# Preparing the mixer's and the second feed-forward's weights inside the first feed-forward's input stage

## The chip, the cores and the metric

The kernel runs on one NeuronCore of a Trainium2 chip. The metric is device time of one execution in microseconds; the figure of a kernel is the median of repeated runs. Five engines work beside each other and meet only through semaphores: TensorE (PE: matrix products), VectorE (DVE), ScalarE (ACT), GpSimd (POOL) and SyncE (SP, which here only issues DMAs). POOL issues DMAs too. Each engine executes its own list of instructions in the order in which the build wrote it: an instruction that waits holds up all that stand behind it on that engine.

## The reference

One encoder layer on x of 1024 tokens by 1024 features, in float32: two feed-forwards (SwiGLU, inner width 2816) with a token mixer between them. Each sub-layer computes `LN(ALPHA*x + w*(1+gate)*f(x*(1+scale)+shift))` where shift, scale and gate come from a small conditioning product. Cut to what matters here:

```python
def swiglu(h, w_in, w_out):
    gate, up = jnp.split(h @ w_in, 2, axis=-1)
    return (jax.nn.silu(gate) * up) @ w_out

def hybrid_mixer(h, w_in, ..., w_out, ...):
    proj = h @ w_in                      # 1024 x 2560 columns
    glu_a, glu_b, q, k, v = split(proj)  # 512 columns each
    conv_out = silu(LN(depthwise_conv31(glu_a * sigmoid(glu_b)) + conv_b))
    # 4 heads: a = softmax(q1 k1) - lam * softmax(q2 k2); rms_norm(a @ v)
    attn_out = diff_attention(q, k, v, ...)
    return concat([conv_out, attn_out]) @ w_out   # 1024 x 1024
```

## The kernel before

Every float32 operand of a large product is split into two parts of the 32-bit format that TensorE takes at one column per step (`F32R`): a high part, written by a cast on ACT, and a low part, the operand less its high part, by a subtraction on DVE (`split`, L141 and L142). A product is then three matmuls (high*high, high*low, low*high). The feed-forwards' products are also cut by a scheme of Strassen's kind: seven half-size products instead of eight, on sums of quarters of the weights (S1 to S4) and of the activations (T1 to T4).

The stages follow each other: the start (0 to 75 us); the input product of feed-forward 1, in 22 blocks of 128 inner columns (to 490.8); its output product (to 706); the mixer's projections, GLU, k, q and v, with the width-31 convolution on DVE beside them (to 950); attention in 8 query tiles by 4 heads (to 1150); the mixer's output product (to 1242); feed-forward 2's input product (to about 1690) and output product.

In `in_phase`, block j runs seven products in the order 1, 2, 6, 5, 7, 3, 4, each of 12 matmuls, and evacuates each from PSUM by DVE and ACT (`in_steps`: the evacuation of product 7 is L425, that of product 3 L428). During a block the next block's weights are loaded by SP, summed (`in_sums`, into tile `sf`), and split (`sh`, `sl`). After each block `hook(j)` does small jobs of the conditioning. After product 2 of the last block the output phase's first step, and after product 5 the second and third, are prepared ahead (`out_ahead`); `out_phase` goes on with steps of 12 matmuls `fo<-wr,gl` (L571), each of which needs a split weight piece `wr` and a split activation piece `gl`.

The projections load raw weights (`kr`, `qr`, `vr`, 512 KB each) and split them. `q_stack` makes the query tiles for the transposes on PE (`qTh` and `qTl`, L1057): its `qh` and its copy of `ql` are POOL instructions, behind the rotary embedding `rope` on the same engine. In attention a worker written as interleaved generators computes per iteration scores, softmax, the difference `p` (POOL, L1128 and L1129, or DVE, L1126), transposes `aT` and the product with v (L1146). `finish` normalises: `ss` on DVE (L1162), `pow` on POOL (L1165), `o` on DVE (L1168). `out_weights` loads a piece of the mixer's output weights, multiplies it with `gate1` (L1099, on POOL for the pieces loaded in attention) and splits it. `gate1` itself is accumulated in the first output phase (`ada_gate`, L155).

The order of feed-forward 2's first blocks is written out by hand in the string `MSEQ`: a token such as `r1G` (right-hand sums of quarter 1, engine G = POOL or V = DVE), `X0GV` and `x0V` (sums S1, S2 of block 0, and their split), `p01` (product 1 of block 0); a leading `!` ties a token to the matmuls before it.

Of the kernel before, what the change touches and what calls it, by code (L numbers as in the profile page):

```python
# [17 lines left out]
P = 128  # L18
T = 1024
# [19 lines left out]
MSEQ = "m5 G0 f0 r0V f1 d5 r1G !m6 f2 r2V f3 d6 r3G m7 d7 F0 !X0GV x0V | !Y0VG p01 p02 s0GV y0V F2 G1 t0V F1 s1VV t1G s2VV p11 !F3 !X1GV s3VV b0 t2V t3V u0GV b1 v0V u1GG v1V b2 b3 !p12 Y1GG u3VV u2GV v2V v3V x1V !p06 y1G p05 !p16 !p07 p15 !p03 !p17 p04 W0 p13 !p14"  # L39
# [11 lines left out]
def layer_kernel(ctx, tc, a, out):  # L51
# [55 lines left out]
    def late_consts(wp, tag, bufs):  # L107
        vec_raw = wp.tile([45, P], F32, tag=tag, bufs=bufs, name="vec_raw")
# [6 lines left out]
        SY.dma_start(cw_raw, a["conv_w"][0])  # L115
        cps = bank("consts_ps")
# [8 lines left out]
        SY.dma_start(ropec, a["rope"].rearrange("(t p) e i -> p t e i", p=P))  # L125
        lraw = wp.tile([P, 4, 64], F32, tag=tag, bufs=bufs, name="lraw")
        for n, nm in enumerate(("lambda_q1", "lambda_k1", "lambda_q2", "lambda_k2")):
            SY.dma_start(lraw[:, n], a[nm].partition_broadcast(P))
        V.tensor_tensor(lraw[:, 0], lraw[:, 0], lraw[:, 1], ALU.mult)
# [162 lines left out]
    def new_ops():  # L292
# [4 lines left out]
        "ra": ([P, 3, 4, P], 2), "rb": ([P, 4, P], 2), "ah": ([P, 3, 4, P], 2), "al": ([P, 3, 4, P], 2),  # L297
# [11 lines left out]
    def in_load(wp, s, w_in, j, q=SY):  # L309
        rp = raw_pool.get(s, wp)  # L310
        ra = rp.tile([P, 3, 4, P], F32, tag="ra", bufs=2, name=f"ra{s}_{j}")
        rb = rp.tile([P, 4, P], F32, tag="rb", bufs=2, name=f"rb{s}_{j}")
# [3 lines left out]
        for dst, src in ((ra[:, 0], k1[:, :, g]), (ra[:, 1], k2[:, :, g]), (rb, k1[:, :, u]), (ra[:, 2], k2[:, :, u])):  # L316
            q.dma_start(dst, src)
        return ra, rb

    def in_gate(wp, s, j, raws):  # L320
        ra, rb = raws
# [5 lines left out]
    def in_sums(wp, s, j, raws, left, eng=V, order=(0, 1)):  # L327
        ra, rb = raws
        if s == 2 and order == (0, 1) and j in (1, 2):
            eng = G  # L330
        if order[0] == 0:
            left["sf"] = [wp.tile([P, 2, 4, P], F32, tag="sf", bufs=2, name=f"sf{s}_{j}_{i}") for i in range(2)]
        sf = left["sf"]
        if 0 in order:
            eng.tensor_tensor(sf[0][:, 0], rb, ra[:, 2], ALU.add)
            eng.tensor_tensor(sf[0][:, 1], sf[0][:, 0], ra[:, 0], ALU.subtract)
        if 1 in order:
            eng.tensor_tensor(sf[1][:, 0], ra[:, 0], rb, ALU.subtract)
            eng.tensor_tensor(sf[1][:, 1], ra[:, 1], sf[0][:, 1], ALU.subtract)
        for i in order:  # L340
            sh = wp.tile([P, 2, 4, P], F32R, tag="sh", bufs=3, name=f"sh{s}_{j}_{i}")
            sl = wp.tile([P, 2, 4, P], F32R, tag="sl", bufs=3, name=f"sl{s}_{j}_{i}")
            last = split(sh, sl, sf[i])
            for e in range(2):
                left[f"S{2 * i + e + 1}"] = (sh[:, e], sl[:, e])
# [19 lines left out]
    late = []  # L365
    pe_last = []
# [7 lines left out]
    def in_steps(wp, s, j, L, ops, gd, begun={}):  # L374
# [32 lines left out]
        def p2():  # L407
            V.tensor_tensor(c0, prod("A12", "B21"), cp["p1"], ALU.add)  # L408
# [9 lines left out]
        def p5():  # L418
            cp["b"] = prod("S1", "T1")
            S.copy(temp("p5"), cp["b"])  # L420
# [6 lines left out]
        def p3():  # L427
            V.tensor_tensor(c1, prod("S4", "B22", cp["b"]), cp["u2"], ALU.add)  # L428
            S.activation(c1, c1, AF.Silu)
# [31 lines left out]
        def p4():  # L461
# [4 lines left out]
            V.tensor_tensor(c0, c0, c21, ALU.mult)  # L466
# [1039 lines left out]
```

## Time and profile before

| | |
|---|---|
| median of 3 runs | 1909.49 us (1908.7 to 1911.0) |
| the profiled execution | 1910.44 us, span 1908.6 us, so 1.84 us outside the span |
| mean granted clock of TensorE | 0.989 of full |
| PE busy | 1825.0 us, 96% of the span; 83.6 us idle |
| DVE / ACT / POOL busy | 1450.6 / 781.3 / 298.2 us |

The engine with the highest share is PE, and its idle time is small, so a change can win only what PE waits for (83.6 us at most) and what it loses at half its clock. The other engines matter where PE waits for one of them, and where one of them is so full that it would make PE wait if it got more to do.

### The profile page before, as it was taken

The numbers are of one execution on the slowest core, as the hardware profiler recorded it, in microseconds if no ns is written. First come the engines' busy times: TensorE is split into PE (matmuls) and PEld (weight loads), VectorE is DVE, ScalarE is ACT, GpSimd is POOL, SyncE is SP. The second block draws the span as 40 slices with busy tenths as digits, with TensorE's granted clock in tenths as the row PEclk, the third lists the DMA queues.
The fourth block names the chain that finished last, engine by engine and source line by source line (L and its number), as shares of the span: only waits on it lengthen the run. The fifth ranks groups of instructions, "written<-read, shape, count | busy, mean of one in ns | idle before, by whom it ended". The sixth has DMA issues, their size and how long they took to land. (4 is left out here: it accounts for less than half of the span.)

```text
span 1908.6 us, 23158 instructions
## 1 busy us (share of the span) xinstructions
PE 1825.0 (96%) x8570; PEld 1513.0 (79%) x8570; DVE 1450.6 (76%) x1952; ACT 781.3 (41%) x1270; POOL 298.2 (16%) x243
## 2 busy tenths in 40 slices
PE   5999999999999999999999789979999999999997
PEld 5788888888888878878788677857888888888886
DVE  4977767766698878999888768688777565569888
ACT  2633333333445442132277664353333333254540
POOL 0000000000000020057667541260000000000001
PEclk9999999999999999999999999989999999999999
DMA  9337445542885325110000014125555333178432
GB/s 311 95 120 224 157 149 177 165 139 90 307 300 157 106 61 166 44 41 27 11 1 1 12 45 154 67 67 170 165 173 180 121 115 123 43 280 284 128 121 72
DMA packets 203952, 246.77 MB, mean 129 GB/s; under 512 B 14378, under 2 KB 125087, under 8 KB 203838
## 3 DMA queue, kind: packets, MB, share of 16 engines
q1 hardware_dynamic: 198378, 234.76, 37.8%
q0 software_dynamic: 2112, 7.34, 1.0%
q10 hardware_dynamic: 3348, 3.18, 0.5%
q8 instruction: 67, 1.10, 0.2%
q14 instruction: 47, 0.39, 0.1%
HBM read 188.08 MB, written 57.15 MB: 128 GB/s over the span
## 5 line engine op out<-in xcount | busy, mean ns | idle before, releaser
L571 PE MATMUL fo<-wr,gl 128*128 128x512 f32 x1848 | 422.5, 390 | 0.5 <-DVE pv L614 0.4
L571 PEld LDWEIGHTS fo<-wr,gl 128*128 128x128 f32 x1848 | 346.2, 188 | 74.7 <-issue 1.0
L142 DVE TENSOR_TENSOR sl<-sf,sh 128x1024 fp32r<-128x1024 f32 x87 | 108.3, 1245 | 110.2 <-ACT sh L141 110.1
L141 ACT CAST sh<-sf 128x1024 fp32r<-128x1024 f32 x88 | 92.8, 1055 | 207.4 <-issue 23.7
L949 DVE SCALAR_TENSOR_TENSOR cacc<-u,convw,cacc 128x1009 f32<-128x1009 f32 (+14 forms) x120 | 151.5, 1324 | 0.2
L381 POOL DMA_DIRECT2D gd<-gf x8 | 4.6, 571 | 887.9 <-DVE gf L447 887.5
L142 DVE TENSOR_TENSOR gl<-gr,gl 128x512 fp32r<-128x512 f32 x148 | 102.1, 695 | 8.5 <-ACT gl L141 6.9
L141 ACT CAST gl<-gr 128x512 fp32r<-128x512 f32 x148 | 90.5, 617 | 24.4 <-DMA gr<-gd 17.6
L155 DVE SCALAR_TENSOR_TENSOR ada<-adaw,c_act,ada 128x512 f32<-128x512 f32 x98 | 73.3, 748 | 28.4 <-DMA adaw<-in_w_ada_dram 27.6
L1075 DVE TENSOR_REDUCE mx<-sc 128x1 f32<-128x1024 f32 x64 | 76.3, 1215 | 19.6 <-PE sc L1073 19.6
L1077 ACT ACTIVATE p<-sc,mx 128x1024 f32<-128x1024 f32 x64 | 71.6, 1121 | 44.7 <-DVE mx L1075 44.5
L141 ACT CAST ah<-ra 128x1536 fp32r<-128x1536 f32 x44 | 65.2, 1481 | 56.0 <-DMA ada<-in_w_ada_dram 12.2
L217 POOL TENSOR_TENSOR rr<-rv,mhalf 128x1 f32<-128x1 f32 x24 | 21.9, 911 | 410.0 <-DVE rv L215 410.0
L409 ACT ACTIVATE gf<-gf 128x512 f32<-128x512 f32 x44 | 27.8, 632 | 125.9 <-DVE gf L408 120.1
L142 DVE TENSOR_TENSOR al<-ra,ah 128x1536 fp32r<-128x1536 f32 x44 | 77.1, 1752 | 1.1 <-ACT ah L141 1.0
L141 ACT CAST wr<-wa 128x512 fp32r<-128x512 f32 x66 | 41.2, 624 | 74.0 <-PE fo L571 72.6
L930 PE MATMUL glu<-hm,gluh 128*128 128x512 f32 x256 | 65.6, 391 | 0.0
L142 DVE TENSOR_TENSOR wr<-wa,wr 128x512 fp32r<-128x512 f32 x66 | 45.6, 690 | 26.1 <-ACT wr L141 25.7
L1129 POOL TENSOR_TENSOR p<-p,p 128x1024 f32<-128x1024 f32 x27 | 65.0, 2408 | 1.8
L1146 PE MATMUL av<-vf,aT 128*128 128x128 f32 x512 | 64.2, 280 | 1.0 <-ACT cacc L1211 1.0
L141 ACT CAST wr<-wb 128x512 fp32r<-128x512 f32 x66 | 40.2, 621 | 60.0 <-PE fo L571 49.6
L1146 PEld LDWEIGHTS av<-vf,aT 128*128 128x128 f32 x512 | 61.3, 196 | 1.5 <-ACT cacc L1211 1.3
(3425 smaller groups left out, 4701.4 us busy)
## 6 DMA issues: line engine op xcount, KB each, us to landing
gr<-gd SPq DMA_DIRECT2D x148, 256.0 KB
ra<-in_ffn_w_in_dram SPq DMA_DIRECT2D x129, 256.0 KB
adaw<-in_w_ada_dram SPq DMA_DIRECT2D x56, 512.0 KB
gd<-gf SPq DMA_DIRECT2D x102, 256.0 KB
wb<-in_ffn_w_out_dram SPq DMA_DIRECT2D x44, 256.0 KB
wa<-in_ffn_w_out_dram SPq DMA_DIRECT2D x44, 256.0 KB
rb<-in_ffn_w_in_dram SPq DMA_DIRECT2D x43, 256.0 KB
gd<-s SPq DMA_DIRECT2D x40, 256.0 KB
```

Of the source, the lines that this page charges most:

```text
L141: a = S.copy(hi, x)
L142: b = eng.tensor_tensor(lo, x, hi.bitcast(F32), ALU.subtract)
L155: V.scalar_tensor_tensor(acc, raw[:, jj], c_act[:, n : n + 1], acc, ALU.mult, ALU.add)
L217: G.tensor_tensor(r, v, mhalf[:, 0:1], ALU.pow)
L409: S.activation(c0, c0, AF.Silu)
L571: PE.matmul(ps, lhsT=g[:, x, ts_], rhs=w[:, y], start=n in (1, 2, 3) and k == i == 0, stop=k == NK - 1 and i == 2, skip_group_check=n not ...
L930: PE.matmul(q[2 * m + h], lhsT=w[:, m * P : (m + 1) * P], rhs=hm[k][h][:, x], start=k == 0 and n == 0, stop=k == KD - 1 and n == 2,)
L949: V.scalar_tensor_tensor(acc[:, lo_t:hi_t], u[:, lo_t + sh : hi_t + sh], convw[:, i, jj : jj + 1], acc[:, lo_t:hi_t], ALU.mult, ALU.add,)
L1075: V.tensor_reduce(mx_, ps, axis=AX.X, op=ALU.max, negate=True)
L1077: S.activation(pe, ps, AF.Exp, bias=mx_, accum_out=sm[:, e : e + 1])
L1129: last = G.tensor_tensor(p0, p0, p1, ALU.add)
L1146: PE.matmul(ps[:, 0:P], lhsT=aT[:, kt], rhs=vf[kt][:, h * P : (h + 1) * P], start=kt == 0, stop=kt == 7)
```

## The change

It prepares pieces of later weights during blocks 2 to 21 of the first input stage and keeps the results in DRAM. There are 48 units of 128 rows by 512 columns: 24 of the mixer's k, q and v columns, 16 halves of its output weights (multiplied by `gate1`), and 8 pieces of the sums S1 to S4 for blocks 0 and 1 of feed-forward 2. A unit is loaded into one of two buffers `mw`, changed in place, cast (ACT), subtracted (DVE) and stored; loads and stores are issued by POOL. Two units are loaded after each of blocks 1 to 10, none after 11, one after 12, and from block 13 one after product 5 and two at the block's end; they are worked off at the next such place.

Later the split pairs are loaded from DRAM by SP: 24 loads of 512 KB in place of 12 for k, q and v, 8 of 1 MB each for the output weights (two of 512 KB per piece) in place of raw pieces of 512 KB, and 6 of 512 KB for the sums (tokens `S0`, `S1`, `T1` in `MSEQ`). The splits and gate multiplications there go, and so do tile `sf` and the sums' own instructions.

The rest: the first stage's sums are made in place in one tile `r4`; `late_consts` is spread over blocks 11 to 13; `gate1` is accumulated after blocks 3 and 5 and no longer in the output phase; the rotary embedding of query tile 0 is on DVE, its `qh` on ACT and both halves of `ql` on DVE; the small `ss` operation of `finish` and its like in `conv_stat` go from DVE to POOL; in `MSEQ` the right-hand sums and splits `r1`, `r3`, `t1` and the second operand of `s0` go from POOL to DVE.

```diff
-MSEQ = "m5 G0 f0 r0V f1 d5 r1G !m6 f2 r2V f3 d6 r3G m7 d7 F0 !X0GV x0V | !Y0VG p01 p02 s0GV y0V F2 G1 t0V F1 s1VV t1G ...
+MSEQ = "m5 G0 f0 r0V f1 d5 r1V !m6 f2 r2V f3 S0 d6 r3V m7 d7 F0 | p01 p02 s0VV F2 G1 t0V F1 s1VV t1V ... T0 S1 ...
...
+        if s == 0:
+            for i in order:
+                if i == 0:
+                    eng.tensor_tensor(ra[:, 2], rb, ra[:, 2], ALU.add)
+                    eng.tensor_tensor(rb, ra[:, 0], rb, ALU.subtract)
+                    eng.tensor_tensor(ra[:, 0], ra[:, 2], ra[:, 0], ALU.subtract)
+                else:
+                    eng.tensor_tensor(ra[:, 1], ra[:, 1], ra[:, 0], ALU.subtract)
...
+        hook(1)
         for j in range(2, NJ):
...
             for n in (1, 2, 6, 5, 7, 3, 4):
                 st[n]()
+                if n == 5 and mid_hook:
+                    mid_hook(j)
...
             hook(j)
+        hook(NJ)
...
+        def mix_part():
+
+            t, dst, *hs = loaded.pop(0)
+            with tc.issue_after(pace["V"]), tc.issue_after(pace["S"]):
+                if hs and hs[0] is None:
+                    sums_of(t[:, 0].rearrange("p (s n) -> p s n", s=4))
+                elif hs:
+                    V.tensor_tensor(t[:, 0], t[:, 0], mods["gate1"][:, hs[0]], ALU.mult)
+                S.copy(t[:, 1].bitcast(F32R), t[:, 0])
+                V.tensor_tensor(t[:, 0].bitcast(F32R), t[:, 0], t[:, 1], ALU.subtract)
+            if hs and hs[0] is None:
+                for x in range(2):
+                    G.dma_start(dst[:, x], t[:, x].rearrange("p (s n) -> p s n", s=4))
+            else:
+                G.dma_start(dst, t)
...
+            pieces({11: 0, 12: 1}.get(j, 2))
+
+        def mid_hook(j):
+            if j > 12:
+                pieces(1)
+
+        def pieces(n):
+            while loaded:
+                mix_part()
+            for _ in range(n):
+                if units:
+                    mix_load()
...
-                raw = wp.tile([P, 2, H], F32, tag="raw", bufs=3, name=f"{name}r{q}")
-                src = mix_in[q * 256 : (q + 1) * 256, col : col + H].rearrange("(k p) n -> p k n", p=P)
-                SY.dma_start(raw, src)
...
-                split(hi, lo, raw)
+                src = mwi[col // H - 2][q * 256 : (q + 1) * 256].rearrange("(k p) x n -> p k x n", p=P)
+                for x, w in enumerate((lo, hi)):
+                    SY.dma_start(w.bitcast(F32), src[:, :, x])
...
+                for x in range(2):
+                    S.copy(qh[:, :, x], qf[t])
+                for x in range(2):
+                    V.tensor_tensor(ql[:, :, x], qf[t], qh[:, :, x].bitcast(F32), ALU.subtract)
...
-        eng.tensor_tensor(raw, raw, gate1, ALU.mult)
...
-        split(*mo_w[j], raw)
+        for w, x in zip(mo_w[j], (1, 0)):
+            SY.dma_start(w.bitcast(F32).rearrange("p (h n) -> p h n", h=2), mwo[j][:, :, x])
...
-            V.tensor_scalar(ss, ss, 1.0 / P, EPS, ALU.mult, ALU.add)
-            yield
+            G.tensor_scalar(ss, ss, 1.0 / P, EPS, ALU.mult, ALU.add)
...
+            elif c in "ST":
+                i = int(c == "T")
+                parts = []
+                for x, tag in ((1, "sh"), (0, "sl")):
+                    parts.append(wp.tile([P, 2, 4, P], F32R, tag=tag, bufs=3, name=f"{tag}2_{k}_{i}"))
+                    SY.dma_start(parts[-1].bitcast(F32), mws[k][:, x, i::2])
...
```

On DVE, where the first input stage ends and the output phase begins, the rows of before are these (`gf_21`, `s_0_21` are the last block's results; `wr` and `gl` are the pieces of the output phase's fourth and following steps):

```order
L457 TENSOR_TENSOR gf_20_3503<-s_0_21_3712,gf_20_3503 128x512
L469 TENSOR_TENSOR s_0_21_3729<-gf_21_3609,gf_20_3503 128x512
L142 TENSOR_TENSOR wr_3769<-wb_3764,wr_3769 128x512
L142 TENSOR_TENSOR gl_3766<-gr_3762,gl_3766 128x512
L142 TENSOR_TENSOR gl_3776<-gr_3772,gl_3776 128x512
```

and those of the change at the same place, where L871 to L874 are the sums and L885 the subtraction of a unit:

```order
L484 TENSOR_TENSOR s_0_21_3993<-gf_21_3854,gf_20_3715 128x512
L873 TENSOR_TENSOR mw<-mw 128x128
L885 TENSOR_TENSOR mw<-mw 128x512 x2
L871 TENSOR_TENSOR mw<-mw 128x128
L872 TENSOR_TENSOR mw<-mw 128x128
L873 TENSOR_TENSOR mw<-mw 128x128
L874 TENSOR_TENSOR mw<-mw 128x128
L885 TENSOR_TENSOR mw<-mw 128x512
L145 TENSOR_TENSOR wr_4062<-wb_4057,wr_4062 128x512
L145 TENSOR_TENSOR gl_4059<-gr_4055,gl_4059 128x512
```

The last three units now stand ahead of the output phase's `wr` and `gl` (left out between the first two rows are the rest of the two units' sums).

POOL at the same place, in the change (before, its rows here are the six stores `gd` alone):

```order
L888 DMA mws_103<-mw 128x4x128 x2
L864 DMA mw<-in_ffn_w_in_dram 128x2x128 x4
L396 DMA gd_10_168<-gf_21_3854 128x512
L396 DMA gd_10_157<-s_0_21_3993 128x512
L888 DMA mws_103<-mw 128x4x128 x4
L864 DMA mw<-in_ffn_w_in_dram 128x2x128 x2
L888 DMA mws_103<-mw 128x4x128 x2
```

The load of the last unit stands behind the stores of the two units before it, whose buffers are the only two (four more `gd` stores are left out).

POOL in the second half of attention, before (`p` is the difference of an iteration, `r` the `pow` of `finish`, `mor` an output weight piece):

```order
L1129 TENSOR_TENSOR p_9066<-p_9066,p_9075 128x1024
L1165 TENSOR_TENSOR r_9161<-ss_8877,mhalf 128x4
L1099 TENSOR_TENSOR mor_9163<-mor_9163,gate_3738 128x1024
L1128 TENSOR_SCALAR p_9132<-p_9132,c_9172 128x1024
L1129 TENSOR_TENSOR p_9123<-p_9123,p_9132 128x1024
```

and in the change:

```order
L1213 TENSOR_TENSOR p_9288<-p_9288,p_9297 128x1024
L1246 TENSOR_SCALAR ss_9102<-ss_9102 128x4
L1248 TENSOR_TENSOR r_9331<-ss_9102,mhalf 128x4
L1212 TENSOR_SCALAR p_9356<-p_9356,c_9391 128x1024
L1213 TENSOR_TENSOR p_9347<-p_9347,p_9356 128x1024
```

The multiplication with the gate has left POOL's list, and a small `ss` has come in.

## Rows read from the trace of the kernel before

**Rows 1.** The page, part 1: busy time of each engine.
```profile
PE 1825.0 (96%) x8570; PEld 1513.0 (79%) x8570; DVE 1450.6 (76%) x1952; ACT 781.3 (41%) x1270; POOL 298.2 (16%) x243
```
**Rows 2.** Windows, one block (15): busy us of PE, PEld, DVE, ACT, POOL; clock.
```profile
357.10:376.20 19.10, 19.10 (x90) 15.92 (x89) 14.91 (x22) 6.42 (x8) 0.00 (x0) 1.00 0.57 182
```
**Rows 3.** Timeline of PE where the output phase begins: start, length, group.
```profile
490.77 29.40 PE L571 MATMUL fo<-wr,gl 128*128 128x512 f32 x129
```
**Rows 4.** Timeline of DVE, same place.
```profile
493.02 0.69 DVE L469 TENSOR_TENSOR s<-gf,gf 128x512 f32<-128x512 f32 x1
493.63 0.69 DVE L142 TENSOR_TENSOR wr<-wb,wr 128x512 fp32r<-128x512 f32 x1
```
**Rows 5.** The page, part 5: groups, busy us, mean ns, idle before.
```profile
L142 DVE TENSOR_TENSOR sl<-sf,sh 128x1024 fp32r<-128x1024 f32 x87 | 108.3, 1245 | 110.2 <-ACT sh L141 110.1
...
L381 POOL DMA_DIRECT2D gd<-gf x8 | 4.6, 571 | 887.9 <-DVE gf L447 887.5
...
L141 ACT CAST gl<-gr 128x512 fp32r<-128x512 f32 x148 | 90.5, 617 | 24.4 <-DMA gr<-gd 17.6
```
**Rows 6.** DMA issues of POOL's queue: size, median us from issue to landing.
```profile
spill<-x POOLq DMA_DIRECT2D x8, 512.0 KB, 3.0
...
gd<-gf POOLq DMA_DIRECT2D x8, 256.0 KB, 3.8
```
**Rows 7.** Waits of PE, 706 to 925 us: total, times, longest.
```profile
PE kT L1021 <- DVE khl L142: 2.6, 2, 2.3
```
**Rows 8.** Waits of PE, 925 to 950 us.
```profile
PE qTh L1057 <- POOL qh L1044: 2.8, 1, 2.8
PE qTl L1057 <- POOL ql L1045: 1.4, 1, 1.4
```
**Rows 9.** Windows of 25 us, columns as in Rows 2.
```profile
925.00:950.00 25.00, 20.71 (x95) 16.87 (x93) 17.54 (x17) 6.96 (x12) 10.68 (x10) 0.86 0.00 1
...
1075.00:1100.00 25.00, 18.76 (x122) 15.80 (x122) 21.23 (x25) 15.70 (x36) 14.78 (x10) 0.93 0.06 22
1100.00:1125.00 25.00, 18.28 (x112) 15.79 (x111) 15.67 (x18) 15.27 (x35) 15.13 (x9) 0.86 0.06 21
1125.00:1150.00 25.00, 22.53 (x170) 20.20 (x169) 15.79 (x24) 19.95 (x47) 5.53 (x4) 1.00 0.21 69
...
1250.00:1275.00 25.00, 18.67 (x80) 14.06 (x79) 21.05 (x16) 14.62 (x20) 17.48 (x11) 0.90 0.36 106
1275.00:1300.00 25.00, 22.12 (x82) 17.39 (x83) 24.26 (x24) 11.97 (x15) 7.79 (x5) 0.86 0.16 53
```
**Rows 10.** Waits of PE, 1050 to 1150 us.
```profile
PE aT L249 <- POOL p L1129: 6.7, 2, 6.0
...
PE aT L249 <- DVE r L1122: 2.5, 1, 2.5
```
**Rows 11.** Timeline of POOL in attention.
```profile
1108.00 2.36 POOL L1099 TENSOR_TENSOR mor<-mor,gate 128x1024 f32<-128x1024 f32 x1
```
**Rows 12.** Waits of PE, 1150 to 1242 us.
```profile
PE mo L1313 <- DVE x L1319: 1.4, 1, 1.4
```
**Rows 13.** Waits of PE, 1242 to 1330 us.
```profile
PE fi_0A L360 <- DVE r_2t1l L142: 3.1, 1, 3.1
PE fi_0A L360 <- POOL r_1t1l L142: 2.9, 1, 2.9
...
PE fi_1S L360 <- DVE sl L142: 1.7, 1, 1.7
```
**Rows 14.** Timeline of DVE at the start of feed-forward 2.
```profile
1259.82 0.69 DVE L1353 TENSOR_TENSOR r_1t<-h,h 128x512 f32<-128x512 f32 x1
...
1263.46 2.83 DVE L1353 TENSOR_TENSOR r_2t<-h,h 128x512 f32<-128x512 f32 x1
```
**Rows 15.** Timeline of POOL, same place.
```profile
1262.47 3.27 POOL L142 TENSOR_TENSOR r_1t1l<-r_1t,r_1t1h 128x1024 fp32r<-128x1024 f32 x1
```
**Rows 16.** Windows of 2 us after PE's longest wait in attention, columns as in Rows 2.
```profile
1118.00:1120.00 2.00, 2.00 (x7) 1.48 (x6) 0.46 (x1) 0.00 (x0) 0.00 (x0) 0.50 0.00 0
```

More of the change, by code (lines that the diff above doesn't have):

```diff
@@ L676, in layer_kernel @@
     x_in = a["x"][0]
+    mix_in = a["mix_w_in"][0]
+    mwi = [dram.tile([D, 2, H], F32, name=f"mwi{g}", tag="mwi", bufs=3) for g in range(3)]
+    mws = [dram.tile([P, 2, 4, 4, P], F32, name=f"mws{j}", tag="mws", bufs=2) for j in range(2)]
+    mwo = [dram.tile([P, 2, 2, H], F32, name=f"mwo{j}", tag="mwo", bufs=8) for j in range(8)]
     with pool("p1a") as wp:
-        in_tags(wp, "ra rb ah al sf sh sl")
+        in_tags(wp, "r4 ah al mw sh sl")
         ops = new_ops()
@@ L829, in layer_kernel, with mix_load @@
         gate_at = (16, 18)
+        gate1_at = (3, 5)
         todo = {}
-        def hook(j):
-            if j == 3:
-                late_consts(wp, "ra", 2)
+        loaded = []
+        def mix_load():
+            src, *rest = units.pop(0)
+            t = wp.tile([P, 2, H], F32, tag="mw", bufs=2, name="mw")
+            if isinstance(src, tuple):
+                r = t[:, 0].rearrange("p (s n) -> p s n", s=4)
+                for dst, x in zip((r[:, 0::3], r[:, 1:3]), src):
+                    G.dma_start(dst, x)
+            else:
+                G.dma_start(t[:, 0], src)
+            loaded.append((t, *rest))
@@ new lines, in layer_kernel @@
+        units = []
+        for g in (1, 0, 2):
+            for k in range(KD):
+                ks = slice(k * P, (k + 1) * P)
+                units.append((mix_in[ks, (g + 2) * H : (g + 3) * H], mwi[g][ks]))
+        for j in range(8):
+            for h in range(2):
+                hs = slice(h * H, (h + 1) * H)
+                units.append((a["mix_w_out"][0, j * P : (j + 1) * P, hs], mwo[j][:, h], hs))
+        w2 = a["ffn2_w_in"][0].rearrange("(k e p) (s n) -> k e p s n", e=2, p=P, s=2)
@@ new lines, in layer_kernel @@
+        for j in range(2):
+            for k in range(4):
+                units.append((tuple(w2[k, e][:, :, j * P : (j + 1) * P] for e in range(2)), mws[j][:, :, :, k], None))
+        def hook(j):
+            if j in gate1_at:
+                n = gate1_at.index(j)
+                if n == 0:
+                    mods["gate1"] = rows.tile([P, D], F32, tag="gate1", name="gate1")
+                with tc.issue_after(pace["Y"]):
+                    todo[j + 1] = ada_gate(wp, raw_slot, 1, 1.0, mods["gate1"], n)
+            if j == 11:
+                todo["consts"] = late_consts(wp, "mw", 2)
+            if 11 <= j <= 13:
+                with tc.issue_after(pace["V"]), tc.issue_after(pace["Y"]):
+                    next(todo["consts"], None)
@@ L844, in hook @@
                 todo.pop(j)()
-        gd = in_phase(0, wp, a["ffn1_w_in"][0], a["ffn1_w_out"][0], ops, early, hook)
-    gate1 = rows.tile([P, D], F32, tag="gate1", name="gate1")
-    mix_in = a["mix_w_in"][0]
+            pieces({11: 0, 12: 1}.get(j, 2))
[8 more added lines that the diff above has]
+                    mix_load()
+        gd = in_phase(0, wp, a["ffn1_w_in"][0], a["ffn1_w_out"][0], ops, early, hook, mid_hook)
     spill1 = [dram.tile([P, D], F32, name=f"spill1_{t}", tag="spill1", bufs=NT) for t in range(NT)]
@@ L1236, in layer_kernel @@
             if i in (22, 26):
-                with tc.issue_after(last):
-                    out_weights(wp, (i - 22) // 4, G)
+                out_weights((i - 22) // 4)
         for c in "f 00 01 10 11 b a 20 21 30 31".split():
```

130 lines of the change are left out of this document (58 added, 72 removed).

## The prediction

> **What bounds the kernel now.** First the page's busy times: PE works 96% of the span [rows 1], so the time is PE's work plus 83.6 us of waiting plus what it loses at half clock. Next, windows: in the first input stage PE has no gap and the clock is full [rows 2], so nothing can be won there, only lost. The waits and the 25-us windows then show where the 83.6 us lie: among others at the first query [rows 8], in the second half of attention [rows 9, 10] and at the start of feed-forward 2 [rows 9, 13]. A wait costs twice: after the wait of 6.0 us on POOL's `p` [rows 10] the granted clock stands at 0.50, the 1.2 GHz level, with PE busy all the time [rows 16]. A window of 25 us with mean clock c lost 25 x (1-c) us of work by that.
>
> The sum is made on the profiled execution, 1910.44 us (span 1908.6 and 1.84 outside it), 0.95 us above the median of the runs; I take the sum off the median, 1909.49.
>
> **The change part by part.**
>
> *Units in the first input stage.* From block 13 a block gets three units: 3 subtractions of 0.69 us, for the gated ones 3 multiplications of the same shape, together 4.1 us of DVE, and 3 casts of 0.62, 1.9 us of ACT [rows 4, 5]. Block 15 has 14.91 us of DVE and 6.42 of ACT in 19.10 [rows 2]: 19.0 and 8.3 after. DVE is then full for a block, but it has had slack in the blocks before. The dearer thing is waiting: a unit's operations stand in DVE's and ACT's lists ahead of a block's evacuations, and behind a store and a load on POOL's queue. Each takes 3.0 to 3.8 us to land [rows 6] after an issue of 0.57 [rows 5]. Between product 5 and the block's end lie three products, 36 matmuls of 29.40/129 = 0.228 us [rows 3], 8.2 us; in them two units must be cast and subtracted (2.6 us), one stored and the next one loaded into its place (7.1 to 8.7 us with the issues). That is 1.5 to 3 us too long; in the lists the late unit's operations stand some two evacuations behind the place, which takes up most of it, so I estimate 0 to 1 us of waiting in each of the blocks, and up to 2 us if what is queued behind it (the evacuation of product 7, whose PSUM bank product 4 wants 2.7 us later) is late. No row of before shows a load in this place. Bounds 0 and +16 (8 blocks by 2); nothing can be gained, as PE has no gap here. I take **+4**, nearer to the end that the full PE of [rows 2] with DVE at 78% suggests.
>
> *The end of that stage.* PE begins the output phase at 490.77 [rows 3] with three prepared steps of 12 matmuls, 8.2 us; the fourth step, at 499.0, needs `wr` and `gl`, which before were made from 493.63 on, directly behind the last block's results [rows 4]. After, three units stand ahead of them on DVE, and three casts on ACT. Units 6 and 7 of the 8 sums are loaded behind the stores of the two before them, whose subtractions stand just ahead of the evacuation of product 7; that product ends two products before 490.77, at 485.3, and a store and a load with their issues, 7.1 to 8.7 us, bring them to about 493.5. Then 8 small sums (between 0.16 and 0.69 us each, the second the size of [rows 4] and four times larger; I take 0.25) and two subtractions, 3.4 us, end at about 497. Then four store issues of 0.57 us, 3.0 to 3.8 us to land, two load issues, 3.0 to 3.8 us to land: 505 to 507 at the most, a us less where the issues overlap the landing. Four sums, cast, subtraction, 2.3 us; then `wr` needs its own cast and subtraction, 1.3 us: 507.5 to 509.5. PE waits 8.5 to 10.5 us and runs some 5 us at half clock, 2.5 us. Bounds: +3, if stores and loads land in 1 us as no row shows, and +18, if unit 6's load is late as well. I take **+12**.
>
> The Trainium skill, "DMA: Bandwidth & Descriptors" (Anatomy of one DMA), gives a DMA issued by POOL about 2.0 us plus its bytes at 436 GB/s: 2.6 us for 256 KB, 3.2 for 512 KB. The rows agree for the larger and have 3.8 for the smaller, with the queue's neighbours beside it. By the page this term would be an estimated 2 us smaller, +10.
>
> *Elsewhere in the first feed-forward.* `gate1`'s accumulation moves from the output phase into blocks 3 and 5; PE waits in neither, 0.
>
> *Projections.* 12 splits of 1.25 us [rows 5] and their casts go, 15 us of DVE; PE waited 2.6 us for DVE's `khl` [rows 7], of which part goes. Twice the bytes by SP are hidden, 12 MB over 220 us. Bounds 0 and -2.6: **-1**.
>
> *First query.* The waits of 2.8 and 1.4 us [rows 8] are for POOL, which does the rotary embedding of tile 0 and then `qh` and `ql`. Now DVE and ACT do it. The `ql` pair stands behind the last convolution operations on DVE; with 15 us of splits gone these end earlier, and I estimate the pair ready about when PE wants it, as DVE's list is a dozen us shorter there. In the window 925 to 950 PE idles 4.3 us and loses 25 x 0.14 = 3.5 to the clock [rows 9]; 7.8 us is the upper bound. Lower bound -2, if the 15 us were only idle time on DVE and the new wait is for `ql`. **-5**.
>
> *Attention, 1075 to 1125.* POOL's gate multiplication, 2.36 us [rows 11], stands ahead of the next `p` and beside DVE, which doubles in time; PE waited 6.7 us for POOL's `p` and 2.5 for DVE's `r` [rows 10]. In the two windows PE idles 6.24 + 6.72 us and loses 1.75 + 3.5 to the clock, 18.2 together; the next window, without such loads, idles 2.47 at full clock [rows 9]. Put that in place of both: 18.2 - 4.9 = 13.3. `ss` of `finish` comes to POOL, some 1 us per query tile, in front of `pow`; POOL has room (15 of 25 us). Bounds -8 (the two waits less a part that the rest of the iteration takes up) and -18. I take **-13**.
>
> *Mixer's output.* The four remaining gate multiplications and splits go; PE waited 1.4 us there [rows 12]. The loads are twice as large and must wait for buffers of attention; the first two groups of products cover them. Bounds +2 (a load that is late) and -3: **-2**.
>
> *Feed-forward 2.* The two windows from 1250 idle 6.33 + 2.88 us and lose 2.5 + 3.5 to the clock, 15.2 together [rows 9]. Of the waits [rows 13] those for POOL's `r_1t1l` and for `sl` go: the sums are loaded, and the POOL operations that stretch DVE's go to DVE: `r_2t` took 2.83 us beside POOL's `r_1t1l` (3.27) where `r_1t` took 0.69 alone [rows 14, 15]. That for `r_2t1l` ends earlier, as DVE's list loses the stretching: the 21 and 24 us of DVE in the two windows [rows 9] shrink by an estimated third. What stays: the chain of DVE still ends last for the early products, and the loads of `S0` wait for a buffer that the first products free, so that product S may want them a us or two before they land. Bounds -4 and -15: **-9**.
>
> Sum: +4 +12 -1 -5 -13 -2 -9 = -14. **1895 us.**
>
> **The rivals.**
>
> *A, the tail is hidden.* If unit 8's chain ends before 499, or the list lets `wr` and `gl` go first, the +12 falls to +2, and with FFN blocks at +2 the sum is -26: 1883 us. For it: 8.2 us of prepared work on PE. Against it: two DMA trips in a row on one queue.
>
> *B, the gains do not arrive.* Where a wait on POOL goes, the next in line ends last: in attention the scores' maximum on DVE and the exponent on ACT, at feed-forward 2 the loads. If attention gives only -8, the first query -2 and feed-forward 2 -4, the sum is +4 +12 -1 -2 -8 -2 -4 = -1 to, with a tail of +8, -5: 1904 us. For it: DVE 21 of 25 us in one of the windows [rows 9]. Against it: the calm window after.
>
> *C, the units make blocks late.* If each store and load lands in 4 us or more rather than 3, all blocks from 13 wait 2 us: +16, and the tail +18 as it is the same chain; with the gains -30 the sum is +4: 1914 us, slower. It decides from about 1 us above the landing times of [rows 6]. Against it: the DMA engines are 57% busy in block 15, the last number but one of [rows 2], so not full.
>
> *D, issues by POOL are held up.* POOL's operations and DVE's with two inputs stretch each other two to three times [rows 14, 15]. If POOL's issue of a DMA were stretched as its `r_1t1l` is, from 0.57 to 1.5 us beside a DVE that is 80% busy, each unit's chain of four issues would be 3.7 us longer: +2 us in 9 blocks, +4 in the tail, sum +8: 1917 us. The issues of [rows 5] fell beside a busy DVE and took 0.57 us. The Trainium skill says in "DMA: Bandwidth & Descriptors" (SWDGE vs HWDGE vs iDMA) that POOL writes its descriptors into SBUF, where DVE can lock it out in its two-port modes. No run so far shows a POOL issue held up by it.
>
> **How the numbers follow.** Forecast 0.55, A 0.14, B 0.18, C 0.08, D 0.05. What a measurement can tell from no change is 0.2%, 3.8 us: faster is below 1905.7, slower above 1913.3. The forecast and A are faster, but for 0.03 of the forecast; B is half to two thirds faster (0.11), the rest the same (0.07); C is slower by 0.06 and the same by 0.02, D slower. Faster 0.77, same 0.12, slower 0.11. The range: the forecast's own bounds, 1884 to 1906, by the chances reach down to A, 1880, and up into the same band, 1909.
>
> **What would show it.** In the trace after: PE waits for `wr` or `gl` at about 499 for 8 to 11 us, with three rows of subtractions `mw` before it, and a clock of 0.5 behind; short waits of PE for DVE's `p` evacuation in blocks 13 to 21, or none; no waits for `qh` and `ql` at 928; the stretch 1075 to 1125 shorter by 13 us, and feed-forward 2's start by 9. Wrong would be: no wait at 499 (A); attention as long as before (B); PE idle in every block (C); POOL's DMA issues over 1 us (D).

## The result, and the profile after

The changed kernel takes 1951.47 us (median of 4 runs, 1949.66 to 1954.8) against 1910.24 of the kernel before (1908.7 to 1914.45): ratio 1.0215, interval 1.0203 to 1.0227. It is 2% slower. The forecast was 1895, faster. The profiled execution took 1949.66 us, its span 1947.9.

Part 1 of the page after, in answer to [rows 1]: PE's busy time grew by only 9 us, so 30 of the 39 us by which the span is longer are waiting.

```profile
PE 1834.2 (94%) x8570; PEld 1517.0 (78%) x8570; DVE 1438.5 (74%) x2017; ACT 784.1 (40%) x1296; POOL 320.0 (16%) x344
```

Where the time went is read best from the starts of the same matmuls in the two traces (us from the span's start; the difference grows where the change loses and shrinks where it wins):

| first matmul of | before | after | difference |
|---|---|---|---|
| input stage, block 11 | 275.7 | 277.0 | +1.3 |
| block 14 | 334.7 | 341.6 | +6.9 |
| block 21 | 471.3 | 500.4 | +29.1 |
| output phase | 490.8 | 540.2 | +49.4 |
| its fourth step | 499.0 | 569.5 | +70.5 |
| GLU | 706.5 | 777.9 | +71.4 |
| v projection | 895.5 | 965.4 | +69.9 |
| attention's scores | 938.8 | 1002.4 | +63.6 |
| attention's products with v | 960.3 | 1023.8 | +63.5 |
| mixer's output | 1148.1 | 1200.6 | +52.5 |
| (its last matmul) | 1241.6 | 1291.5 | +49.9 |
| feed-forward 2, block 4 | 1342.1 | 1380.0 | +37.9 |
| (last matmul of all) | 1897.0 | 1936.1 | +39.1 |

So 70 us were lost up to the fourth step of the output phase, and some 33 won behind it, up to feed-forward 2's fourth block. PE's waits over the whole span, longest first (total, times, longest):

```profile
PE fo L590 <- ACT gl L144: 20.8, 1, 20.8
...
PE fi_21A L374 <- ACT p L417: 11.4, 1, 11.4
...
PE fi_21A L374 <- DVE p L440: 3.3, 1, 3.3
PE convw_ps L124 <- DMA cw_raw<-in_conv_w_dram: 3.2, 1, 3.2
...
PE fi_17A L374 <- DVE p L440: 1.9, 1, 1.9
```

The first is the wait for the output phase's fourth step, which the prediction placed there with 8.5 to 10.5 us; the two of `fi_21A` stand in the last block, and `convw_ps` is the transpose of the late constants. The ones like `fi_17A`, in blocks 14 to 19, are waits for evacuations (`p`, L417 on ACT and L440 on DVE). The windows of the last block and of the tail behind it show PE idle and the clock down (columns as in [rows 2]):

```profile
500.00:525.00 25.00, 13.58 (x47) 10.30 (x46) 6.63 (x15) 4.65 (x9) 6.69 (x10) 0.73 0.50 162
525.00:550.00 25.00, 20.43 (x78) 16.09 (x76) 11.59 (x27) 4.04 (x8) 9.69 (x15) 0.86 0.61 201
550.00:575.00 25.00, 5.49 (x14) 4.24 (x15) 8.18 (x17) 6.02 (x12) 8.15 (x9) 0.52 0.44 137
```

In blocks 14 to 20 the same matmuls took 136.60 us before and 158.80 after. The first row is of before, the second of after, the third the stretch behind a wait in block 17:

```profile
334.70:471.30 136.60, 136.60 (x610) 112.75 (x608) 92.74 (x130) 44.00 (x55) 0.00 (x0) 1.00 0.41 133
...
341.60:500.40 158.80, 144.31 (x609) 113.99 (x609) 119.64 (x182) 55.73 (x77) 25.09 (x44) 0.98 0.65 221
...
431.00:433.00 2.00, 2.00 (x7) 1.60 (x6) 1.39 (x2) 0.06 (x1) 0.00 (x0) 0.58 1.00 329
```

Of the 22.2 us, PE idles for 14.5. In the other 7.7 its matmuls take longer: behind a wait the clock falls while PE is busy, in the third row to a mean of 0.58.

How an evacuation comes late is seen on DVE in block 17 (timeline: start, length, group, in brackets the idle time before it and what ended it):

```profile
426.17 0.69 DVE L883 TENSOR_TENSOR mw<-mw,gate 128x512 f32<-128x512 f32 x1 [1.80 <-DMA mw<-in_mix_w_out_dram]
426.77 1.22 DVE L145 TENSOR_TENSOR sl<-r,sh 128x1024 fp32r<-128x1024 f32 x1
427.91 1.28 DVE L885 TENSOR_TENSOR mw<-mw 128x512 fp32r<-128x512 f32 x2
429.12 0.68 DVE L440 TENSOR_TENSOR p<-fi_17A,p 128x512 f32<-128x512 f32 x1
```

and on PE at the same time:

```profile
429.85 0.50 PE L374 MATMUL fi_17A<-r_0t3h,ah 128*128 128x512 f32 x1 [1.90 <-DVE p L440]
```

DVE waits 1.80 us for a unit's load, does what stands next in its list, and reaches the evacuation of product 7 with PE already waiting. Over blocks 14 to 20 DVE waits for units' loads ten times (total, times, longest):

```profile
DVE mw L883 <- DMA mw<-in_mix_w_out_dram: 19.5, 10, 4.4
```

The transfers of the units (the page's DMA issues on POOL's queue, in answer to [rows 6]) take longer than the rows of before:

```profile
mwi<-mw POOLq DMA_DIRECT2D x24, 512.0 KB, 5.6
...
mwo<-mw POOLq DMA_DIRECT2D x16, 512.0 KB, 4.7
...
mw<-in_mix_w_in_dram POOLq DMA_DIRECT2D x24, 256.0 KB, 4.6
...
mw<-in_mix_w_out_dram POOLq DMA_DIRECT2D x16, 256.0 KB, 4.2
mws<-mw POOLq DMA_DIRECT2D x16, 256.0 KB, 2.7
```

By these medians a store and a load are 8.9 to 10.2 us of landing, where 6.0 to 7.6 had been reckoned, and single transfers scatter: the stores `mwo` of blocks 14 to 20 landed in 2.9 to 8.1 us. The sums' stores look quick, but POOL's timeline where the last block begins shows something else:

```profile
495.15 0.76 POOL L888 DMA_DIRECT2D mws<-mw  x1 [1.48 <-issue]
498.21 0.76 POOL L888 DMA_DIRECT2D mws<-mw  x1 [2.30 <-DVE mw L874]
501.25 0.75 POOL L888 DMA_DIRECT2D mws<-mw  x1 [2.27 <-ACT gf L444]
504.85 0.76 POOL L888 DMA_DIRECT2D mws<-mw  x1 [2.85 <-issue]
505.60 0.71 POOL L864 DMA_DIRECT2D mw<-in_ffn_w_in_dram  x1
```

From one store to the next pass 3.0 us or more, though the issue itself is shown with 0.76; the load behind the last store follows at once. It is the same in the tail, where DVE has nothing to do from 551.5 to 566.45 us and no row names anything that POOL waits for:

```profile
554.21 0.76 POOL L888 DMA_DIRECT2D mws<-mw  x1 [2.40 <-issue]
557.24 0.75 POOL L888 DMA_DIRECT2D mws<-mw  x1 [2.27 <-issue]
560.26 0.76 POOL L888 DMA_DIRECT2D mws<-mw  x1 [2.27 <-issue]
...
566.45 0.29 DVE L871 TENSOR_TENSOR mw<-mw 128x128 f32<-128x128 f32 x1 [14.97 <-DMA mw<-in_ffn_w_in_dram]
```

The last row is the first sum of the last unit. The output phase's `wr` and `gl` stand behind it, and PE starts the fourth step at 569.5.

The gains are where they were forecast. PE has no wait left at the first query [rows 8]; of POOL's `p` in attention [rows 10] nothing is left, and of feed-forward 2's waits [rows 13] little (waits of PE, 1290 to 1380 us):

```profile
PE hT L1366 <- ACT x L236: 2.0, 2, 1.8
PE fi_1S L374 <- DMA sh<-mws: 1.8, 1, 1.8
PE fi_0A L374 <- DVE r_3bl L145: 0.8, 1, 0.8
```

### The profile page after: what moved, and what is told of

It is laid out like the page before. It is cut to its first block, busy times and chain, and to the rows that moved or that the text cites. A ratio compares the mean times of both kernels' runs of the same rounds, so it can differ in the third digit from the quotient of the medians.

```text
span 1947.9 us, 23568 instructions
## 1 busy us (share of the span) xinstructions
PE 1834.2 (94%) x8570; PEld 1517.0 (78%) x8570; DVE 1438.5 (74%) x2017; ACT 784.1 (40%) x1296; POOL 320.0 (16%) x344
## 4 chain that ended last, share of the span: by engine, by line
PE 69%; DVE 9%; issue 7%; DMA 7%; POOL 4%; ACT 3%; SPq 0%; POOLq 0%; DVEq 0%; ACTq 0%
PE fo L590 19%; PE glu L1012 4%; PE mo L1394 4%; PE vp L1059 2%; PE kp L1059 2%; DMA mwo<-mw 2%; ACT p L1164 1%; PE fi_4A L374 1%; PE fi_6A L374 1%; PE fi_2A L374 1%; PE fi_10A L374 1%; PE qp L1059 1%; PE fi_5A L374 1%; PE fi_3A L374 1%; PE fi_11A L374 1%
## 5 line engine op out<-in xcount | busy, mean ns | idle before, releaser
L1031 DVE SCALAR_TENSOR_TENSOR cacc<-u,convw,cacc 128x1012 f32<-128x1012 f32 (+14 forms) x120 | 151.0, 1321 | 0.2
L145 DVE TENSOR_TENSOR sl<-sf,sh 128x1024 fp32r<-128x1024 f32 x40 | 48.9, 1223 | 59.0 <-ACT sh L144 59.0
L1164 ACT ACTIVATE p<-sc,mx 128x1024 f32<-128x1024 f32 x64 | 71.4, 1118 | 37.0 <-DVE mx L1162 36.9
L144 ACT CAST sh<-sf 128x1024 fp32r<-128x1024 f32 x40 | 42.2, 1054 | 105.8 <-PE fi_16S L374 5.8
L424 ACT ACTIVATE gf<-gf 128x512 f32<-128x512 f32 x44 | 27.8, 632 | 100.5 <-DVE gf L423 94.7
L884 ACT CAST mw<-mw 128x512 fp32r<-128x512 f32 x48 | 28.7, 617 | 96.9 <-DVE mw L874 54.8
L145 DVE TENSOR_TENSOR sl<-r,sh 128x1024 fp32r<-128x1024 f32 x44 | 53.6, 1220 | 14.9 <-ACT sh L144 14.7
L145 DVE TENSOR_TENSOR wr<-wa,wr 128x512 fp32r<-128x512 f32 x66 | 45.4, 688 | 25.6 <-ACT wr L144 25.6
L444 ACT ACTIVATE gf<-gf 128x512 f32<-128x512 f32 x44 | 27.7, 629 | 86.3 <-DVE gf L443 86.2
```

Of the source, the lines that this page charges most:

```text
L144: a = S.copy(hi, x)
L145: b = eng.tensor_tensor(lo, x, hi.bitcast(F32), ALU.subtract)
L1031: V.scalar_tensor_tensor(acc[:, lo_t:hi_t], u[:, lo_t + sh : hi_t + sh], convw[:, i, jj : jj + 1], acc[:, lo_t:hi_t], ALU.mult, ALU.add,)
L1164: S.activation(pe, ps, AF.Exp, bias=mx_, accum_out=sm[:, e : e + 1])
```

## The experiments

All comparisons are with the kernel before on the same chip. "Attention" is the stretch from the first product with v to the mixer's output: 187.8 us before, 176.8 after.

**e1, the layout of the sums' stores.**

```diff
-    mws = [dram.tile([P, 2, 4, 4, P], ...)]      # hi/lo, sum, piece
+    mws = [dram.tile([P, 4, 2, 4, P], ...)]      # piece, hi/lo, sum
-                for x in range(2):
-                    G.dma_start(dst[:, x], t[:, x].rearrange("p (s n) -> p s n", s=4))
+                G.dma_start(dst, t.rearrange("p x (s n) -> p x s n", s=4))
```

> The changed kernel with the 8 sum units stored in another layout: the piece index first, so that a unit is one store of 4 KB runs per partition instead of two stores of 512-byte runs (the later loads of the sums become two of 256 KB each in 512-byte runs instead of one in 2 KB runs). Theory 1 (POOL's queue can issue such a 512-byte-run store only every 3.07 us, and the units of block 21 and of the tail stand behind it): block 21's loss of 20 us falls to about 5, that between the output phase's third and fourth step from 21 to about 10; together -26, about 1925 us. Theory 2 (the place of the units and the length of store plus load is the cause, whatever the layout): -6 at the most, about 1946. Feed-forward 2's start 0 to +2 for the shorter runs of the loads.

Measured: 1928.26 us, ratio 1.0084 (1.0061 to 1.0107). The last block's loss fell from 20.3 to 10.8 us and that before the fourth step from 21.1 to 7.5. POOL's timeline shows two stores in one go,

```profile
526.13 1.23 POOL L887 DMA_DIRECT2D mws<-mw  x2 [7.31 <-DVE mw L885]
```

of 512 KB each, where a store of 256 KB took 3.0 us in the changed kernel. Theory 1 was right on the issue; a little less came back than it said, since in the last block PE still waits 8.6 us for the evacuation of product 7, as in the blocks before it. Why a store of 512-byte runs holds POOL for 3.0 us stays open.

**e2, the constants as before.**

```diff
-            if j == 11:
-                todo["consts"] = late_consts(wp, "mw", 2)
-            if 11 <= j <= 13: ... next(todo["consts"], None)
+            if j == 3:
+                for _ in late_consts(wp, "r4", 2): pass
```

> The changed kernel with the late constants loaded and transposed at block 3 in one go, as before the change, and not in blocks 11 to 13. Theory: the 5.6 us by which block 13 starts late come from PE's transposes of the constants, which wait for their DMA (3.2 us and the half clock behind it) in block 12; then block 13 starts 5 to 6 us earlier and the time is about 1946. Rival: the 5.6 us come from the units and the conditioning in blocks 11 and 12; then it stays within 1 us of 1951.

Measured: 1951.57 us, unchanged (ratio 1.0206). Block 14 starts 7.3 us late as in the changed kernel (6.9), but the loss lies in blocks 4 to 6 now: block 8 starts 7.0 late instead of 1.3. The wait for the constants' DMA goes, blocks 11 to 13 lose only 0.3 us, and other waits for evacuations come in blocks 4 and 5. So the theory had the place right and the remedy wrong; the rival's time came out, but not its reason.

**e3, no sum units; e4, two units per block.** e3 leaves the sum units out and starts feed-forward 2 as before. e4 is e3 with the constants at block 3 and

```diff
-            pieces({11: 0, 12: 1}.get(j, 2))
+            pieces(2)
...
         def mid_hook(j):
-            if j > 12:
-                pieces(1)
+            pass
```

> The changed kernel without the 8 sum units; feed-forward 2 starts as before the change (sums and splits there, same order string). Theory 1: block 21's 20 us and the tail's 21 go whole, feed-forward 2's gain of about 12 is given back: 1951 - 41 + 12 = 1922. Rival (late units of any kind make the last blocks late, the sums only happen to be last): the loss of 2.8 us per block of blocks 14 to 18 stays and the tail keeps 5 to 10 of its 21: about 1930.

Measured: 1924.63 us (ratio 1.0055, 1.0035 to 1.0075). The last block takes 19.5 us and PE goes into the fourth step without a gap, as before the change: both losses there were the sum units'. Blocks 14 to 20 still lose 28 us (in the profiled execution, 1929.6 us, the slowest of four). Feed-forward 2's start is as long as before the change, so the 12 us were won by the loaded sums and the tokens moved with them.

> As the run without sum units, with the late constants at block 3, and the 40 units as two after each of blocks 1 to 20, none after product 5. Theory 1 (a buffer needs a store and a load, about 10 us on POOL's queue, between two uses, and a whole block gives 19 us): no block is late, the gains behind stay (about 21 us without feed-forward 2's start): 1910 + 1 - 21 = 1890. Rival (DVE's and ACT's extra work makes the evacuations late, whatever the DMAs): two thirds of the 22 us of blocks 13 to 20 stay: about 1905.

Measured: 1902.63 us, ratio 0.9953 (0.9937 to 0.9969): faster than before. From block 8 to block 20 next to nothing is lost (6.6 us late at block 8, 7.9 at 20). PE's waits between 320 and 500 us are

```profile
PE fi_17S L374 <- ACT p L435: 0.4, 1, 0.4
PE fi_19A L374 <- DVE p L440: 0.3, 1, 0.3
```

and two of 0.2; neither DVE nor ACT waits for a unit's load in any block. The time is near the rival's, but not for the rival's reason, since blocks 14 to 20 do not keep their loss. 6.6 us are lost by block 8, where the constants stand as in e2, and some 6 more in feed-forward 2's blocks (PE waits 3.0 us in block 9, where the gate's weights come late; before the change 0).

**e5, the work without the transfers.**

```diff
+                if pace["j"] > 11:
+                    V.tensor_tensor(t[:, 1], t[:, 0], mods["gate1"][:, 0:H], ALU.mult)
+                    S.copy(t[:, 1].bitcast(F32R), t[:, 0])
                 S.copy(t[:, 1].bitcast(F32R), t[:, 0])
```

> The kernel with two units per block (e4_two_per_block) in which, from block 12 on, every unit has one more DVE operation and one more ACT cast of the same shape (their results are overwritten), so that two units cost DVE 4.1 us and ACT 2.5 us per block, as three do in the changed kernel, with the DMAs of two. Theory 1 (what makes the blocks late is the wait for store and load, not the engines' work): blocks 13 to 21 start as in e4 within 2 us and the time stays within 3 us of 1903. Rival (the work itself makes the evacuations late): the 2.8 us per block of blocks 14 to 20 come back, some 15 to 20 us: about 1920.

Measured: 1901.18 us (ratio 0.9942), and the blocks start within 2.5 us of e4's. The windows from 320 to 500 us, of e4

```profile
320.00:500.00 180.00, 178.84 (x789) 146.26 (x788) 140.02 (x200) 68.00 (x94) 19.94 (x37) 1.00 0.69 229
```

and of this run

```profile
320.00:500.00 180.00, 178.71 (x793) 146.40 (x792) 149.60 (x218) 78.31 (x112) 19.82 (x36) 1.00 0.69 227
```

show 10 us more on DVE and on ACT, DVE at 83%, and PE as busy as before. The rival falls: this much more work on the engines does not make a block late.

**e13, one buffer.** The reverse of e5: work, units and transfers of e4, but with one buffer a store and a load must fit between two places instead of into a block. Half of the units are worked off after product 5 for it, so the place of the work changes too.

```diff
-        "mw": ([P, 2, H], 2)
+        "mw": ([P, 2, H], 1)
...
-            pieces(2)
+            pieces(1)
         def mid_hook(j):
-            pass
+            pieces(1)
```

> The kernel with two units per block (e4_two_per_block), but with one unit buffer instead of two, one unit worked off and the next loaded after product 5 and one at the block's end: the same 40 units, the same work per block, the same stores and loads; only the time that a store and a load have together falls from a block (19 us) to 10.9 and 8.2 us by turns. Theory (what makes the changed kernel's blocks late is that a store and a load, 8 to 10 us with their issues, do not fit between the two places, and the evacuations stand behind the waiting operations): the blocks lose 1.5 to 3 us each from block 3 on, 25 to 50 us in all: 1928 to 1953. Rival (the trip matters only where DVE is full, or only with three units): no more than e4, about 1903.

Measured: 1963.64 us, ratio 1.0271. The output phase starts 71.5 us late instead of 9.0: 3.1 us more for each of 20 blocks, and in the blocks of the units without a gate too (32.9 us by block 11). DVE in block 15,

```profile
419.98 0.69 DVE L883 TENSOR_TENSOR mw<-mw,gate 128x512 f32<-128x512 f32 x1 [3.30 <-DMA mw<-in_mix_w_out_dram]
...
422.33 0.68 DVE L440 TENSOR_TENSOR p<-fi_15A,p 128x512 f32<-128x512 f32 x1
```

and PE's next start there:

```profile
423.07 0.50 PE L374 MATMUL fi_15A<-r_0t3h,ah 128*128 128x512 f32 x1 [2.80 <-DVE p L440]
```

It is block 17 of the changed kernel over again. Over the blocks DVE and ACT wait for units' loads, where e4 and e5 have no such wait:

```profile
DVE mw L883 <- DMA mw<-in_mix_w_out_dram: 35.5, 15, 8.1
...
ACT mw L884 <- DMA mw<-in_mix_w_in_dram: 68.1, 15, 10.0
```

So it is the time for store and load that makes the blocks late, as the theory said, with somewhat more loss than it allowed. That the place after product 5 adds nothing by itself has no run of its own; the waits just shown are for transfers.

**e6, e9, e10, what attention gained from.** e6 puts one multiplication of 128x1024 on POOL back at the two places; e9 the whole preparation of the four pieces; e10 only the normalisations' small operations on DVE.

```diff
 e6, e9, after the combination of iterations 22 and 26
+                    junk = wp.tile([P, D], F32, tag="raw", bufs=2, name=f"junk{i}")
+                    G.tensor_tensor(junk, mods["gate1"], mods["gate1"], ALU.mult)   # e6
+                    out_weights_raw(wp, (i - 22) // 4, G)                           # e9
 e10
-            G.tensor_scalar(ss, ss, 1.0 / P, EPS, ALU.mult, ALU.add)
+            V.tensor_scalar(ss, ss, 1.0 / P, EPS, ALU.mult, ALU.add)
+            yield
```

> The kernel with two units per block (e4_two_per_block) in which, at the two places in attention where before the change an output weight piece was multiplied with the gate on POOL, POOL makes one multiplication of 128x1024 again (of the gate with itself, its result unused). Theory (the 12 us that attention became shorter are this multiplication in front of the next difference, and DVE's stretching beside it): attention from the first product with v to the mixer's output is 8 to 13 us longer than in e4 and the time about 1912. Rival (the gain is from the split and casts that left DVE and ACT, or from the small operations of the normalisation): 0 to 3 us longer.

> The kernel with two units per block (e4_two_per_block) in which the four output weight pieces that attention prepares are made as before the change: raw load, multiplication with the gate (two on POOL, two on DVE), cast on ACT, subtraction on DVE. Theory (attention became 12.7 us shorter because the whole chain load, multiplication, cast, subtraction left the engines' lists; the multiplication alone, e6, was worth 2.6): attention from the first product with v to the mixer's output is 8 to 13 us longer than in e4. Rival (the gain is from the small normalisation operations that went to POOL): 3 us longer, as in e6.

> The kernel with two units per block (e4_two_per_block) in which the small operations of the normalisations (mean plus epsilon) are on DVE again, each its own step of the generator, as before the change. Theory (the output weights' chain is attention's gain): attention within 2 us of e4. Rival: 6 to 12 us longer.

Measured: 1905.69, 1912.12 and 1899.41 us; attention 177.7, 184.7 and 171.6 us where e4 has 175.1. In the nine runs with the change's own attention the stretch takes 174.8 to 176.8 us, so differences of 2 us say nothing. The multiplication alone brings back 2.6 us, hardly more than that and against my theory for e6, though e6's takes 1.90 us where the real one takes 2.38 in e9. With load, cast and subtraction 9.6 come back (in a profiled execution 3 us above e9's median). In e9 PE's old waits are there again, near those of [rows 10] (1040 to 1150 us):

```profile
PE aT L252 <- POOL p L1215: 3.6, 3, 2.1
...
PE aT L252 <- DVE r L1208: 2.6, 1, 2.6
```

And the small operations are worth 3.5 us the other way (e12 has them on DVE too, and 171.7 us): that part of the change was a loss. e9 still lacks 3.1 us of the 187.8 of before although it carries that loss, so some 6 us of attention's gain have no run that shows their cause.

**e7, the first query alone,** on the kernel before (the lines of `rope`, `q_evac` and `q_stack` as in the change).

> The kernel before with the first query alone changed: rotary embedding of tile 0 on DVE, its high parts on ACT, its low parts on DVE. Theory (the wait was for POOL's chain): PE's 4.2 us of waits at the first query go with the half clock behind, -4 to -7 us: 1904 to 1906. Rival (the gain needs the room on DVE that the projections' splits leave): then the low parts stand behind the convolution and the query comes no earlier: 0 to -2.

Measured: no change, ratio 0.9998 (0.9989 to 1.0007); the scores start 0.7 us earlier. The wait has only changed its name:

```profile
PE qTl L1063 <- DVE ql L1051: 2.7, 1, 2.7
```

The rival is right in that the first query's part alone wins nothing: PE now waits for the low parts on DVE. That the splits gone from DVE make the rest of the 6.3 us is the likely reading; no run takes the splits away alone.

**e8, e11, e12, a version that keeps the gains.** e8: sum units first, in e1's layout, then k, q, v and half of the output weights, two per block, with the constants at block 3; the other half of the output weights is prepared in the mixer's output as before.

```diff
-        gate1_at = (3, 5)
+        gate1_at = (7, 9)
...
-        for j in range(8):          # output weight halves as units
+        for j in range(4):
```

e11 adds buffers of their own for the constants and feed-forward 2's gate two blocks later; e12 is e8 with that gate and e10's normalisation.

> A version meant to keep the gains: the 8 sum units first (stored in 4 KB runs), then the 24 of k, q and v, then 8 halves of the output weights, two after each of blocks 1 to 20; the gate is accumulated after blocks 7 and 9 and the late constants at block 3; the last four pieces of output weights are made in the mixer's output as before. Theory 1: no late blocks, first input stage +1 to +3, nothing at its end; projections and first query -8, attention -11 to -13, feed-forward 2's start -10 to -12, mixer 0: about 1882. Rival (gain of feed-forward 2 needs the output weights prepared too, and the early blocks are made late by the sums): about 1895.

> The candidate (e8_candidate) with the late constants in buffers of their own (so that they neither take one of the two weight buffers nor wait for a unit's), loaded after block 3, transposed a block later, and feed-forward 2's gate accumulated after blocks 12 and 15 instead of 10 and 13. Theory (in every version with units the constants cost 4 to 6 us because they share two buffers with weights or units): blocks 5 to 8 lose 0 to 1 us instead of 4.3, feed-forward 2's blocks 0 to 2 instead of 3.6, time 1886 to 1889. Rival (DVE is too full in blocks 4 and 5 with units and conditioning): 1892 to 1894.

> The candidate (e8_candidate) with the normalisations' small operations on DVE again (worth 3.5 us of attention in e10) and feed-forward 2's gate accumulated after blocks 12 and 15 (worth 2.7 us in e11). Theory (both are independent of the rest): 1894 - 6 = 1888. Rival (they win what other waits take back): 1892 to 1895.

Measured: 1894.37 (ratio 0.9902, 0.9885 to 0.9920), 1897.94 (0.9937) and 1886.17 us (0.9868, 0.9852 to 0.9885). e8 missed its 1882: its first stage ends 13.3 us late, not 1 to 3. Of these, 2.7 are lost by block 5, 4.3 in block 5 and 2.5 in block 17; in these two blocks PE waits 2.4 and 2.2 us for an evacuation on ACT; whether the constants or the fuller lists of the early blocks delay it is not shown. In e11 block 5 starts on time (0.2 us late instead of 2.7), but PE then waits 8.1 us for a conditioning sum whose weights are loaded late, and block 6 starts 9.5 us late, more than the 7.0 of e8. So what the constants cost, and by which chain, differs with the place and stays open. e12 beats both kernels; it is 25.6 us under the one before, which took 1911.76 beside it.

## Why the prediction was wrong

*What held.* The terms behind the output phase: projections -1.5 (forecast -1), first query -6.3 (-5), attention -11.0 (-13), mixer's output -2.6 (-2), feed-forward 2's start -12.0 (-9). Together -33 where -30 was said. Their working fits what the traces show, with an exception: attention's -11.0 came out near the forecast partly by luck. It was put down to POOL's multiplication in front of the next `p`. That by itself is worth about 2.6 us (e6); the whole preparation, with load, cast and subtraction, is worth 9.6 (e9); and the small `ss` operation, for which POOL was said to have room and nothing was charged, cost 3.5 (e10). The rest has no run. For the first query e7 agrees with the condition that the prediction set, that DVE's list be shorter.

*What failed: the units in the first input stage.* The forecast was "+4, bounds 0 and +16". Of the 49.4 us by which the output phase starts late, 22.2 are blocks 14 to 20, 20.3 the last block, 5.6 the late constants, and 1.3 lie before block 11. The working had the right quantity, a store, a load and 2.6 us of work between two places 8.2 us apart, which is 1.5 to 3 us too long. The step that failed is the next one, by which the late unit's place in the lists "takes up most of it" and leaves 0 to 1 us of waiting per block. PE waited 2.1 us in each of blocks 14 to 20 and lost 1.1 more to the slower matmuls behind the waits, which this term leaves out although the prediction says elsewhere that a wait costs twice. And PE has no gap in which a late block could catch up, so each block's lateness adds to the last one's. e13, with the units and the work of e4, loses 3.1 us more per block.

The landing times were too low as well, 3.0 to 3.8 us against medians of 4.2 to 5.6 in the changed kernel, but they are not what decides. In blocks 14 to 20 of e13 the gated units' stores and loads have medians of 3.2 and 3.5 us, inside the prediction's range, and PE idles there for 14.5 us all the same, as in the changed kernel:

```profile
377.50:534.00 156.50, 141.97 (x608) 112.81 (x607) 112.74 (x161) 52.20 (x70) 15.73 (x29) 0.99 0.58 193
```

"Bounds 0 and +16" with eight blocks at 2 us was the sum of a number that the working itself had put at up to 3.

*The last block and the tail.* +12 was forecast for the tail, +21 measured, and the last block's +20 was not foreseen. The mechanism of the tail was right, two trips on POOL's queue ahead of `wr` and `gl`; the term that was mis-sized is its four store issues of 0.57 us each. The sums' stores went out 3.0 us apart, and the second trip, reckoned at 8 to 10 us, took 15.0 (DVE's idle time before 566.45). The first trip also ended some 4 us later than reckoned, 6.7 us into the output phase instead of 2.7. Both losses are the sum units' (e3), and about half of the 41 us is POOL's issue of stores in 512-byte runs, which [rows 5] could not show: their 0.57 us are of stores in long runs (e1 gives 23 us back).

*Not in the sum.* The late constants: +5.6 in blocks 11 to 13, where a transpose on PE waits 3.2 us for a load. The prediction passed over this edit.

*The rivals.* C, "the units make blocks late", is what happened, with 1914 for a price that was 37 us too low: its 2 us of waiting per block are right, but it leaves out the slower matmuls, the last block and the constants. Its condition, landing times of 4 us or more, came about but was not needed, as e13 shows. A is refuted, and B too, since the gains came in full. D named POOL's issue, and the sums' stores are indeed held up, but not by DVE: between 551.5 and 561 us DVE is idle and they still go out 3.0 us apart, and in e1 two stores of long runs go out in 1.23 us. The sign that the prediction gave for D, issues over 1 us, would not have found it, as the issue's own row shows 0.76. (D also says that POOL's and DVE's operations stretch each other two to three times; for the DVE operation [rows 14] have 0.69 and 2.83 us, four times.) The lockout by DVE that the Trainium skill ("DMA: Bandwidth & Descriptors", SWDGE vs HWDGE vs iDMA) speaks of is therefore not what holds the stores of the tail, and the rows shown here have no sign of it. The estimate by the Trainium skill for the transfers ("DMA: Bandwidth & Descriptors", Anatomy of one DMA: 2.6 us for 256 KB, 3.2 us for 512 KB) is below what the stage measured, 4.2 to 4.6 and 4.7 to 5.6 us, so the measurement decides, and the smaller +10 of that passage was further off.

## What to carry to other kernels

Work slipped into a full stage cost next to nothing here as long as no engine's list waited for its transfers, even with DVE at 83% (e4, e5). So give each transfer a whole period between its issue and its use, and count the store that must free the buffer. A wait of a few us per period that the working shows is not made up by slack in a stage whose first engine has no gap: multiply it by the periods, and add what the lower clock behind each wait costs. Take landing times for a sum from the stage in which the transfer will run, with their scatter, and the time of an issue from stores of the same shape; read it from the distance between two issues, not from the length of one.
